# Splitting streamed weights: the low part from an accumulating transfer instead of a GpSimd subtraction

## The chip, the cores and the metric

The kernel runs on one core of one Trainium2 chip. The core has five engines with a queue each: TensorE (PE, with its weight loads shown as PEld), VectorE (DVE), ScalarE (ACT), GpSimd (POOL) and SyncE (SP), which here issues all transfers. The metric is the device time of one execution in microseconds. Before the change it is 1318.51 us (median of three runs, 1318.17 to 1319.07). The profiled execution, from which all durations below come, took 1321.76 us.

## The reference, cut to what matters

One layer of a hybrid block: 1024 latent tokens and 256 context tokens of width 1024 are normalised and modulated, and go through one input projection `w_in` (1024 x 6176). Its columns feed a gated DeltaNet with 8 heads (q, k, v, their short convolution, a gate z), a multi-scale pooling branch (u and its gate), and per-head decay numbers. An output projection, a gated residual and a last RMSNorm follow.

```
proj = einsum('bld,dp->blp', hn, w_in)              # hn: [1024 or 256, 1024]
qkv, ab, z_dn, u_pool, z_pool = split(proj)
qkv = silu(short_conv(qkv, conv_w)) ...             # 5 taps
o   = gated_delta_rule(q, k, v, g, beta, s0) ...    # context first, then latents from its state
y_pool = pool_mixer(u_pool) * silu(z_pool)
x = x + gate_x * concat(o, y_pool) @ w_out
```

All is float32. The kernel gets near that accuracy from a faster matmul type (float32r, which keeps fewer bits) by splitting each operand into a high part, rounded to float32r, and a low part, the rest: a product is then hi*hi + hi*lo + lo*hi.

## The kernel before, in words

The projection's columns are cut into 64 tiles of 128 columns: 16 for the context (k and v of each head, 256 tokens), 8 for the pooling gate, 32 for the heads (v, k, z, q of each, 1024 tokens) and 8 for u. `order` (line 654) holds their sequence, `SEQ` (line 33) its pattern: the context tiles first, with two of the gate's, then mostly the head tiles, and after the heads the eight u tiles. For each, `w_load` (line 669) brings 512 KB of raw weights to SBUF: for the first 18 tiles into two buffers in turn (`raw2`, which the profile shows as kT, and `wraw`), afterwards into `wraw` alone. `w_split` (line 679) then makes the two parts, in two halves of 4 of the 8 k-blocks. It calls `split` (line 674): ACT copies raw to the high part `whi`, and POOL subtracts, `wlo = raw - whi`. Both are double buffered. `gemm_take` starts the load of tile i+2 as tile i begins (for i below 16).

`gemm_half` (line 734) does a tile's products for up to 512 tokens in one PSUM bank: for each of 8 k-blocks three products (`PASSES`: whi*hi, whi*lo, wlo*hi), so that the third product already reads `wlo`. In its first half of the tokens it also splits the next tile's weights: the first half of the split after product 4, the second after product 14 (of 24), and from i = 16 on it issues the load of tile i+2 right behind. Tiles 0 and 1 are split earlier, between the steps of the modulation (line 1605), and tile 1 splits at products 14 and 18.

The order of all instructions is written out by a small planner, `Flow` (line 70). The gemm is its main thread. The other stages are side threads (generators): conversion and transposition of the latents (`x_half`, `x_split`), convolution of the tiles (`conv_post`), the DeltaNet's stages for two groups of context heads and for eight latent heads (`stage_a`, `stage_b`, `stage_d`, `stage_k`, `stage_q`, the scans). The planner gives each instruction a modelled cost, keeps a clock for each engine, and puts a side step into the program when its modelled inputs are due; flags (`flow.flag`, `yield ("name", n)`) order the threads. It does not model one engine slowing another. After the heads, `mix_all` and `pool_out` do the pooling, and `second_half` (line 1969) prepares the second half of the output projection while the mixing runs.

The profile puts nearly all instructions on line 364, the helper that records them, and transfers on 382; so they are told apart by their tiles: `whi`, `wlo`, `wraw`, `kT`, `vT`, `qT` (convolution results, one convolution instruction reads u and one of these), `hnhi`, `hnlo` (the latents' parts), `D` (decays, and also the context's high part), `dlo`, `ws`, `rp` (pooling).

Of the kernel before, what the change touches and what calls it, by code (L numbers as in the profile page):

```python
# [11 lines left out]
ACTF = mybir.ActivationFunctionType  # L12
ALU = mybir.AluOpType
# [21 lines left out]
N2 = 18  # L35
# [9 lines left out]
WD = 0  # L45
# [3 lines left out]
GROUPS = (2, 1, 3, 0)  # L49
# [15 lines left out]
}  # L65
ISSUE = 1220.0
LANDED = 950.0


class Flow:  # L70
# [210 lines left out]
def _use(ap, write):  # L281

    t = ap.tensor
    name = t.name
    off = int(ap.offset)
    dims = [(int(q[0]), int(q[1])) for q in ap.ap]
    if name.split("_")[0] in PSUM_TAGS:
        return name, 0, P, 0, 1 << 40, True
    if name.split("_")[0] in DRAMS or name.startswith("in_") or name.startswith("out_"):
        return name, 0, 1, off, off + 1 + sum(s * (n - 1) for s, n in dims if s > 0), write  # L290
    row = _size(t)
    p, f = off // row, off % row
    return name, p, p + dims[0][1], f, f + 1 + sum(s * (n - 1) for s, n in dims[1:] if s > 0), write
# [20 lines left out]
class Engine:  # L314
# [44 lines left out]
    def __getattr__(self, op):  # L359
        f = getattr(self.real, op)  # L360

        def call(*a, **k):
            self.flow.spend(self.name, self.cost(op, a, k), self.uses(op, a, k))
            return f(*a, **k)  # L364

        return call


class Queue:
# [21 lines left out]
def kernel(  # L391
# [22 lines left out]
    flow = Flow()  # L414
    pe, act, dve, pool = (Engine(flow, e, n) for e, n in (
        (nc.tensor, "pe"), (nc.scalar, "act"), (nc.vector, "dve"), (nc.gpsimd, "pool")))
    sync = Queue(flow, nc.sync)
# [3 lines left out]
    KT = D // P  # L421
# [111 lines left out]
    for d in range(2):  # L533
        pool.memset(mask[d], 0.0)
        pool.memset(tri[d], 1.0)
        s = 1 if d == 0 else -1
# [14 lines left out]
    ps = pp_tile()  # L551
# [60 lines left out]
    for k in range(KT):  # L612
        mod_part(0, mod_ps[0], k)
        if k == 4:
            ps = pp_tile()
            pe.transpose(ps[:, 0:P], vec_row, ident)
            act.activation(out=vec[:, 16:64], in_=ps[:, 16:64], func=ACTF.Copy)
            ps = pp_tile()
# [48 lines left out]
    raws = {}  # L667

    def w_load(n):
        if n < len(order):  # L670
            t = raws[n] = raw2 if n % 2 and n < N2 else gemm.tile([P, KT, P], FP32, tag="wraw", name="wraw")
            sync.dma_start(out=t, in_=w_in_d[:, :, order[n]:order[n] + P])

    def split(raw, hi, lo, e):

        act.activation(out=hi, in_=raw, func=ACTF.Copy)
        e.tensor_tensor(out=lo, in0=raw, in1=hi, op=ALU.subtract)

    def w_split(n, part):
        if n >= len(order):  # L680
            return
        if part == 0:
            wq[n] = [gemm.tile([P, KT, P], FP32R, tag=f"w{s}", bufs=2, name=f"w{s}") for s in ("hi", "lo")]
        hi, lo = wq[n]
        s = slice(part * (KT // 2), (part + 1) * (KT // 2))
        split(raws[n][:, s, :], hi[:, s, :], lo[:, s, :], dve if n < WD and part else pool)

    arrs = [{a: const.tile([P, 16, n], FP32, name=f"{a}{i}") for a in ("ngc", "neg", "edl", "egl", "beta")}
            for i, n in enumerate((NBC, NB))]
# [44 lines left out]
    def gemm_half(i, w, src, t0, m, evac):  # L734
        ps = mm_tile()
        j = 0
        for k in range(KT):
            for a, b in PASSES:
                pe.matmul(ps[:, 0:m], w[a][:, k, :], src(b, k, t0),
                          start=(j == 0), stop=(j == 3 * KT - 1))  # L740
                j += 1
                if t0 == 0 and j == (4 if i > 1 else 14) and i:
                    w_split(i + 1, 0)
                if t0 == 0 and j == (14 if i > 1 else 18) and i:
                    w_split(i + 1, 1)
                    if i + 2 >= N2:
                        w_load(i + 2)
                yield
        evac(ps[:, 0:m], t0)

    def gemm_tile(src, n, evac):
# [636 lines left out]
    def x_half(hf):  # L1388
        for k in range(KT):
            n = hf * KT + k  # L1390
            yield TAKE
            tp = pp_tile()
            for i in range(4):
                pe.transpose(tp[:, i * P:(i + 1) * P], xs[4 * hf + i][:, k * P:(k + 1) * P], ident)
            if XACT & 4 == 0:
                yield
            if n >= len(TMP):
                yield ("split", n - len(TMP))
            if XACT & 4:
                yield "act"  # L1400
            h32 = dl_tile([P, 512], *TMP[n % len(TMP)])
            act.activation(out=h32, in_=tp, func=ACTF.Identity,
                           scale=md[:, 0, 1, k:k + 1], bias=md[:, 0, 0, k:k + 1])
            flow.give()
            flow.flag("h32", n)
            flow.add(x_split(hf, k, h32), [("h32", n)], True)

    def x_split(hf, k, h32):
        if XACT & 8:
            yield "dve"  # L1410
        dve.tensor_copy(hn[2 * hf][:, k, :], h32)
        yield
        e = dve if k % XD == 0 else pool
        e.tensor_tensor(out=hn[2 * hf + 1][:, k, :], in0=h32, in1=hn[2 * hf][:, k, :], op=ALU.subtract)
        flow.flag("split", hf * KT + k)
# [68 lines left out]
    def thread_a():  # L1484
        for k in (-5, -4, -3):
            flow.flag("merged", k)
            flow.flag("done", k)
        for k in range(-2, H):
            yield ("k", k)
            yield ("ab", k >= 0)  # L1490
            yield ("done", k - 2)
            yield from stage_a(jobs[k])

    def thread_q():
# [334 lines left out]
    def out_main():  # L1829
# [127 lines left out]
        late = []  # L1957
# [10 lines left out]

        def second_half():
            yield ("mixed",)  # L1970
            pl_p.release()
            pools["c"] = Pool(flow, tc.alloc_tile_pool(name="outc", bufs=1, side="right", reuse_waits="tile"))
            wos = {k: [ot2([P, D], f"wo{s}{n}", 1, FP32R) for s in ("hi", "lo")] for n, k in enumerate(KS[:4])}
            yield ("pool", 2)
            for t in range(2):
                y_tiles(t, 1, ot2, 2)
                y_part(t, 1, *PARTS[0])
                wo_load(KS[t], *wos[KS[t]])
            for k in KS[2:4]:
                wo_load(k, *wos[k])  # L1980
            yield ("pool", 3)
            for slot in ("zp0", "zp1"):
                free_raw(slot)
            for t in range(2):
                y_part(t, 1, *PARTS[1])
            for k in KS[4:]:
                wo_load(k, *[pb([P, D], f"d{s}", 4, FP32R) for s in ("hi", "lo")])
            yield ("wo", KS[5])
            closed.update(("zp0", "zp1", "outb"))
            while not closed.issubset(free):  # L1990
                yield ("rel", released[0])
            cols["gate"], cols["fgain"] = gate, fgain = [pb([P, D], "zp", 2) for _ in range(2)]
            sync.dma_start(out=gate, in_=gate_d.partition_broadcast(P))
            sync.dma_start(out=fgain, in_=final_gain.partition_broadcast(P))
            x_load(0)
            x_load(1)
            yield ("heads",)
            y_tiles(2, 1, oa, 3)
            for p in PARTS:
                y_part(2, 1, *p)  # L2000
            y_load(3, 0, oa, 3)
            y_load(3, 1, oa, 3)
# [80 lines left out]
```

## Time and profile before

| what | value |
|---|---|
| median of runs | 1318.51 us |
| profiled execution | 1321.76 us, of which 1320.0 us span |
| PE busy | 1212.5 us (92%) |
| DVE busy | 928.0 us (70%) |
| ACT busy | 570.8 us (43%) |
| POOL busy | 438.7 us (33%), of which wlo<-wraw,whi 158.0 us x110 |
| transfers | 123.73 MB, mean 94 GB/s |
| granted TensorE clock | 0.962 of full speed, mean |

The busy shares are means over stages that have different limits; a stage is read from a window of its own. A timeline row gives start, duration, engine and tiles, and in brackets how long the engine idled before it and what ended that. In a group of instructions the figures after the first bar are the total busy time and the mean of one in ns, those after the second the idle time of the engine just before them and what released it. Where an instruction takes longer than others of its shape, it was held up while it ran; the profile does not say by what, so the rows of the other engines at that moment are put beside it.

### The profile page before, as it was taken

Reading aid. Unit: us, or ns where it says so; the run is one execution under the profiler, and the core shown is the slowest. Engines: PE = TensorE matmul, PEld = TensorE weight load, DVE = VectorE, ACT = ScalarE, POOL = GpSimd, SP = SyncE. Lnnn points to the kernel's source line nnn. Section 1 sums busy time; section 2 is a strip of 40 time slices with the busy share of each in tenths; the row PEclk is TensorE's granted clock in tenths of the full one; section 3 lists DMA queues with packets and bytes.
Section 4 is the critical chain, followed back from the end, with each engine's and each line's share of the span. In section 5 each row is a group of like instructions: output and inputs, shape, how many; then the busy total and the mean of one; then the engine's idle time right before and its main releaser. Section 6 shows DMA issues by size and latency. Waiting matters only on the chain.

```text
span 1320.0 us, 26398 instructions
## 1 busy us (share of the span) xinstructions
PE 1212.5 (92%) x10631; PEld 977.8 (74%) x10631; DVE 928.0 (70%) x1883; ACT 570.8 (43%) x1498; POOL 438.7 (33%) x451
## 2 busy tenths in 40 slices
PE   8876699899899999999999989999999999799997
PEld 2666577677777877788778768778788777688887
DVE  4799989868886787877776867878433999724212
ACT  3466437444436547455474464643613123322110
POOL 2477433230421423314132233141215454402330
PEclk9788899899999999989999999999999899899999
DMA  9533344223121213212221131212313135565230
GB/s 329 188 99 93 86 140 125 74 57 90 37 49 48 78 42 100 58 46 80 49 83 44 41 100 41 69 63 43 103 60 109 48 104 185 199 206 157 83 112 32
DMA packets 157384, 123.73 MB, mean 94 GB/s; under 512 B 47106, under 2 KB 135115, under 8 KB 157261
## 3 DMA queue, kind: packets, MB, share of 16 engines
q1 hardware_dynamic: 157261, 122.04, 30.6%
q8 instruction: 83, 1.36, 0.4%
q14 instruction: 40, 0.33, 0.1%
HBM read 101.43 MB, written 20.60 MB: 92 GB/s over the span
## 4 chain that ended last, share of the span: by engine, by line
PE 40%; DVE 14%; ACT 6%; DMA 2%; issue 2%; POOL 2%; DVEq 0%; SPq 0%; POOLq 0%; ACTq 0%
PE mm L364 24%; PE sc L364 5%; PE o L364 4%; DVE kT L364 4%; PE pp L364 3%; PE pa L364 3%; DVE t L364 3%; DVE ws L364 3%; ACT junk L364 2%; ACT ks L364 1%; DMA D<-gscr 1%; DVE dlo L364 1%; DVE rp L364 1%; POOL wlo L364 1%; DVE zp L364 1%
## 5 line engine op out<-in xcount | busy, mean ns | idle before, releaser
L364 PE MATMUL mm<-hnhi,whi 128*128 128x512 f32 x768 | 321.0, 418 | 0.9 <-ACT whi L364 0.9
L364 PE MATMUL mm<-hnhi,wlo 128*128 128x512 f32 x768 | 316.7, 412 | 2.0 <-POOL wlo L364 2.0
L364 PE MATMUL mm<-hnlo,whi 128*128 128x512 f32 x768 | 316.9, 413 | 0.0
L364 POOL TENSOR_TENSOR wlo<-wraw,whi 128x512 fp32r<-128x512 f32 x110 | 158.0, 1442 | 337.3 <-ACT whi L364 330.5
L364 PEld LDWEIGHTS mm<-hnhi,whi 128*128 128x128 f32 x768 | 147.7, 192 | 26.8 <-issue 1.7
L364 PEld LDWEIGHTS mm<-hnhi,wlo 128*128 128x128 f32 x768 | 146.9, 191 | 26.0 <-POOL wlo L364 2.5
L364 PEld LDWEIGHTS mm<-hnlo,whi 128*128 128x128 f32 x768 | 147.6, 192 | 22.9
L364 DVE SCALAR_TENSOR_TENSOR kT<-u,cw,kT 128x512 f32<-128x512 f32 (+1 forms) x96 | 94.8, 994 | 5.3 <-ACT kT L364 1.8
L364 POOL TENSOR_TENSOR D<-D,mask 128x512 f32<-128x512 f32 x40 | 58.9, 1478 | 92.3 <-DMA D<-gscr 76.8
L364 ACT ACTIVATE y<-sc 128x256 f32<-128x256 f32 (+1 forms) x65 | 24.9, 383 | 131.3 <-PE sc L364 125.3
L364 ACT ACTIVATE u<-mm 128x512 f32<-128x512 f32 (+1 forms) x64 | 34.8, 543 | 88.3 <-PE mm L364 88.1
L364 DVE SCALAR_TENSOR_TENSOR t<-t,laneN 128x1 f32<-128x1 f32 (+4 forms) x150 | 68.0, 453 | 6.8 <-DMA laneN<-ds 2.8
L364 ACT ACTIVATE whi<-wraw 128x512 fp32r<-128x512 f32 x110 | 67.5, 633 | 1.8 <-DMA wraw<-in_w_in_dram 1.5
L364 DVE SCALAR_TENSOR_TENSOR vT<-u,cw,vT 128x512 f32<-128x512 f32 (+1 forms) x80 | 67.2, 843 | 1.5
L364 DVE TENSOR_TENSOR pw<-mm,zp 128x512 f32<-128x512 f32 (+1 forms) x12 | 8.0, 669 | 83.9 <-PE mm L364 83.9
L364 ACT ACTIVATE D<-D,ngc 128x128 f32<-128x128 f32 x160 | 53.1, 403 | 30.7 <-POOL D L364 30.7
L364 DVE SCALAR_TENSOR_TENSOR qT<-u,cw,qT 128x512 f32<-128x512 f32 (+1 forms) x80 | 63.0, 788 | 2.9 <-ACT qT L364 1.2
L364 DVE SCALAR_TENSOR_TENSOR S<-S,egl,sc 128x128 f32<-128x128 f32 x112 | 33.7, 343 | 33.4 <-PE sc L364 30.4
L364 DVE SCALAR_TENSOR_TENSOR r<-sc,neg,vn 128x128 f32<-128x128 f32 x128 | 38.7, 345 | 23.0 <-PE sc L364 22.9
L364 PEld LDWEIGHTS sc<-S,kT 128*128 128x128 f32 x256 | 36.9, 192 | 15.6 <-issue 9.1
L364 PE MATMUL mm<-D,whi 128*128 128x256 f32 x128 | 41.2, 322 | 7.3 <-DVE ks L364 4.5
L364 PE MATMUL sc<-S,kT 128*128 128x128 f32 x256 | 40.7, 282 | 7.2 <-DVE S L364 6.7
(409 smaller groups left out, 2785.5 us busy)
## 6 DMA issues: line engine op xcount, KB each, us to landing
wraw<-in_w_in_dram SPq DMA_DIRECT2D x55, 512.0 KB, 3.8
D<-gscr SPq DMA_DIRECT2D x40, 256.0 KB, 4.1
qd<-escr SPq DMA_DIRECT2D x16, 512.0 KB
kT<-in_w_in_dram SPq DMA_DIRECT2D x9, 512.0 KB, 4.0
whnhi<-in_w_mod_dram SPq DMA_DIRECT2D x8, 512.0 KB, 3.5
whnlo<-in_w_mod_dram SPq DMA_DIRECT2D x8, 512.0 KB, 9.5
D<-in_w_mod_dram SPq DMA_DIRECT2D x8, 512.0 KB, 4.9
yscr<-zs SPq DMA_DIRECT2D x8, 512.0 KB, 2.8
```

What stands on the lines that cost most here:

```text
L364: return f(*a, **k)
```

## The change

The low part is no longer subtracted by POOL. ACT writes the high part, then writes the negated high part into `wlo`, and a transfer issued from POOL's queue adds the raw weights to it in place (SBUF to SBUF, 256 KB, `accum_op=add`). In tiles from 2 on the products are reordered: first the 16 that read `whi`, then the 8 that read `wlo`; the splits of the next tile move from products 4 and 14 to 2 and 8, and with the second one the load of tile i+2 (i of 16 and more). Two threads get one more flag to wait for. The planner gets costs for the new instruction.

```diff
+ADDS = 1000.0
+ADDED = 1500.0
...
+    def add_to(self, out, in_):
+
+        u = [_use(out, True), _use(in_, False)]
+        self.flow.spend(self.name, ADDS, u)
+        self.flow.note("sync", u, self.flow.free[self.name] + ADDED)
+        return self.real.dma_start(out=out, in_=in_, accum_op=ALU.add)
...
-        split(raws[n][:, s, :], hi[:, s, :], lo[:, s, :], dve if n < WD and part else pool)
+        act.activation(out=hi[:, s, :], in_=raws[n][:, s, :], func=ACTF.Copy)
+        act.activation(out=lo[:, s, :], in_=raws[n][:, s, :], func=ACTF.Copy, scale=-1.0)
+        pool.add_to(lo[:, s, :], raws[n][:, s, :])
...
-        for k in range(KT):
-            for a, b in PASSES:
-                pe.matmul(ps[:, 0:m], w[a][:, k, :], src(b, k, t0),
-                          start=(j == 0), stop=(j == 3 * KT - 1))
-                j += 1
-                if t0 == 0 and j == (4 if i > 1 else 14) and i:
-                    w_split(i + 1, 0)
-                if t0 == 0 and j == (14 if i > 1 else 18) and i:
-                    w_split(i + 1, 1)
-                    if i + 2 >= N2:
-                        w_load(i + 2)
-                yield
+        late = [(k, p) for k in range(KT) for p in PASSES[:2]] + [(k, PASSES[2]) for k in range(KT)]
+        for k, (a, b) in late if i > 1 else [(k, p) for k in range(KT) for p in PASSES]:
+            pe.matmul(ps[:, 0:m], w[a][:, k, :], src(b, k, t0),
+                      start=(j == 0), stop=(j == 3 * KT - 1))
+            j += 1
+            if t0 == 0 and j == (2 if i > 1 else 14) and i:
+                w_split(i + 1, 0)
+            if t0 == 0 and j == (8 if i > 1 else 18) and i:
+                w_split(i + 1, 1)
+                if i + 2 >= N2:
+                    w_load(i + 2)
+            yield
...
     def x_half(hf):
...
+        flow.flag("xt", hf)
...
     def thread_a():
...
             yield ("done", k - 2)
+            yield ("xt", 0)
             yield from stage_a(jobs[k])
...
         def second_half():
             yield ("mixed",)
+            yield ("pw", GROUPS[-1])
             pl_p.release()
```

## Rows read from the trace of the kernel before

**Rows 1.** Busy time by stretch (us), all engines; (x) counts instructions.
```profile
core 0: us, PE busy (x) PEld busy (x) DVE busy (x) ACT busy (x) POOL busy (x), PEclk, DMA share, GB/s
50.00:160.00 110.00, 75.35 (x469) 68.03 (x468) 105.74 (x179) 65.70 (x158) 75.26 (x92) 0.87 0.30 85
756.00:845.00 89.00, 82.88 (x897) 68.27 (x896) 68.80 (x161) 46.57 (x137) 26.72 (x27) 0.98 0.22 62
1028.00:1100.00 72.00, 66.32 (x277) 53.51 (x276) 69.68 (x68) 15.76 (x25) 34.95 (x24) 0.95 0.25 77
```

**Rows 2.** Groups of DVE instructions, 50 to 160 us.
```profile
L364 DVE SCALAR_TENSOR_TENSOR kT<-u,cw,kT 128x256 f32<-128x256 f32 x28 | 18.5, 660 | 2.5 <-ACT kT L364 1.8
L364 DVE SCALAR_TENSOR_TENSOR vT<-u,cw,vT 128x256 f32<-128x256 f32 x16 | 15.3, 956 | 0.4
L364 DVE SCALAR_TENSOR_TENSOR qT<-u,cw,qT 128x256 f32<-128x256 f32 x12 | 9.6, 802 | 0.3
L364 DVE CAST hnhi<-XT 128x512 fp32r<-128x512 f32 x4 | 6.2, 1554 | 0.0
...
L364 DVE CAST hnhi<-tmp 128x512 fp32r<-128x512 f32 x4 | 4.0, 1003 | 0.2 <-ACT tmp L364 0.2
...
L364 DVE CAST hnhi<-W 128x512 fp32r<-128x512 f32 x4 | 2.7, 683 | 0.0
...
L364 DVE CAST hnhi<-Y 128x512 fp32r<-128x512 f32 x4 | 2.6, 638 | 0.0
```

**Rows 3.** Timelines of DVE, POOL and SP, 89 to 102 us.
```profile
92.78 4.71 DVE L364 SCALAR_TENSOR_TENSOR vT<-u,cw,vT 128x256 f32<-128x256 f32 x4
97.42 0.41 DVE L364 CAST hnhi<-Y 128x512 fp32r<-128x512 f32 x1
...
100.96 1.52 DVE L364 SCALAR_TENSOR_TENSOR kT<-u,cw,kT 128x256 f32<-128x256 f32 x3
...
94.36 2.85 POOL L364 TENSOR_TENSOR wlo<-kT,whi 128x512 fp32r<-128x512 f32 x2
...
97.24 0.37 SPq L382 DMA_DIRECT2D kT<-in_w_in_dram  x1
```

**Rows 4.** The same stretches, instructions on wlo alone: PE, PEld, POOL.
```profile
50.00:160.00 110.00, 41.20 (x125) 26.59 (x124) 42.14 (x30) 0.87 0.30 85
756.00:845.00 89.00, 26.30 (x64) 12.09 (x64) 10.70 (x9) 0.98 0.22 62
1028.00:1100.00 72.00, 30.26 (x76) 14.53 (x76) 20.25 (x10) 0.95 0.25 77
```

**Rows 5.** Groups of PE and of ACT, 50 to 160 us.
```profile
L364 PE MATMUL mm<-D,wlo 128*128 128x256 f32 x109 | 34.7, 319 | 4.0 <-POOL wlo L364 3.2 <-POOL u L364 0.7
...
L364 ACT ACTIVATE whi<-wraw 128x512 fp32r<-128x512 f32 x16 | 9.7, 621 | 0.0
```

**Rows 6.** Transfers: issuer, count, KB each, median us from issue to landing.
```profile
wraw<-in_w_in_dram SPq DMA_DIRECT2D x55, 512.0 KB, 3.8
D<-gscr SPq DMA_DIRECT2D x40, 256.0 KB, 4.1
...
B<-in_x_dram SPq DMA_DIRECT2D x4, 512.0 KB, 8.4
```

**Rows 7.** Timelines of ACT and PE, 28 to 40 us.
```profile
30.92 1.14 ACT L364 ACTIVATE whi<-wraw 128x512 fp32r<-128x512 f32 x2
...
36.15 0.28 PE L364 MATMUL mm<-D,wlo 128*128 128x256 f32 x1
36.27 0.28 PE L364 MATMUL mm<-D,whi 128*128 128x256 f32 x1
```

**Rows 8.** Chain of waits, 756 to 845 us: start, us, what.
```profile
756.22 1.42 POOL wlo L364
757.64 1.62 POOL sm L364
```

**Rows 9.** Timelines of DVE and POOL, 1028 to 1100 us.
```profile
1048.26 1.16 DVE L364 TENSOR_TENSOR dlo<-ws,dhi 128x1024 fp32r<-128x1024 f32 x1
...
1061.95 2.31 DVE L364 TENSOR_TENSOR dlo<-ws,dhi 128x1024 fp32r<-128x1024 f32 x1
...
1058.87 4.31 POOL L364 TENSOR_TENSOR wlo<-wraw,whi 128x512 fp32r<-128x512 f32 x2 [7.70 <-ACT whi L364]
```

## The prediction

> **What bounds the kernel now.** I began with busy time by stretch, since the shares over the whole span mix stages. It shows three kinds of stage [rows 1]. From 50 to 160 us, where the context tiles and the conversion of the latents run, DVE is busy 105.74 of 110 us and PE only 75.35: DVE bounds the front. In a head's stretch (756 to 845 us; the eight heads repeat it) PE is busy 82.88 of 89 us and DVE 68.80: PE bounds, and 6.1 us a head are idle. From 1028 to 1100 us, the mixing of the pooling branch, DVE is busy 69.68 of 72 us and PE 66.32: DVE again, with PE close behind.
>
> The second view was the groups of DVE instructions in the front [rows 2], because an engine that is busy 96% may be working or held. The reader should compare the mean of a group with an undisturbed one of the same shape. Three convolution steps in a row took 1.52 us, 0.51 us each, where POOL ran nothing large; four of them took 4.71 us, 1.18 each, while POOL subtracted two halves of weights (2.85 us, from 94.36) [rows 3]. A cast of 128x512 took 0.41 us when undisturbed [rows 3], and its four groups have means of 638 to 1554 ns [rows 2]. So POOL's large two-input instructions hold DVE up, and DVE's busy time in the front contains waiting. POOL is busy 75.26 us there [rows 1], 42.14 of it on 30 subtractions for `wlo` [rows 4].
>
> The waits that the change names directly are small: PE waited 3.2 us for `wlo` in the front's context products [rows 5].
>
> **The change part by part.** It removes POOL's subtraction, adds an ACT copy and a transfer for each half tile, and moves the products and splits.
>
> *Front, what POOL gives back to DVE.* The 56 convolution steps of [rows 2] sum to 43.4 us; undisturbed they would take 56 x 0.51 = 28.6, so 14.8 are waiting. The 16 casts sum to 15.5 us against 16 x 0.41 = 6.6: 8.9 more. Together 23.7 us. I give `wlo` its share of POOL's busy time, 42.14 of 75.26 or 56%: 13.3 us. The bounds are 0 (the instruction that issues a transfer holds DVE just as long as the subtraction did) and 23.7 (with fewer large POOL instructions the rest no longer meets DVE either). DVE then needs 105.7 - 13.3 = 92.4 us; at its present 96% the stretch would be 96 us.
>
> What is late next is ACT. It has 65.70 us of work there and gets 30 copies more of 0.621 us [rows 5], 18.6 us: 84.3 of 96, 88% instead of 60%. DVE waits little for ACT at present (2.5 us before its largest group [rows 2]); with a queue that full it will wait more, and I let that take a quarter. Front: **-10 us**.
>
> The Trainium skill (page "SBUF — State Buffer", section "Who interferes with whom") adds what no row here shows: a DVE instruction with two SBUF inputs contends with a GpSimd one that reads SBUF, not with one that only writes it, while a DVE cast in a two-port mode contends with either. The trace agrees with the first half, 1.18 against 0.51 us. By the rule the convolution steps' part of the waiting goes wholly and the casts' part does not: 56% of 14.8, less the same quarter, would make the front -6 instead of -10.
>
> *Start.* Tiles 0 and 1 keep the old order of products, and the first product that reads `wlo` starts at 36.15 us [rows 7]. ACT's eight copies now follow one another from 30.92 us at 0.57 us each (1.14 for two [rows 7]), so the low copy of tile 0's first half ends at 32.1 and that of tile 1's first half, the sixth, at 34.3. The landing of such a transfer is not in the trace. The nearest row is the other one of 256 KB, 4.1 us; beside a busy stream of loads 512 KB took 8.4 us [rows 6]. With 4.1 tile 0 is just in time (36.2) and tile 1, whose first low product comes 12 products of 0.12 us later at 37.6, waits until 38.4; with 8.4 it waits until 42.7. PE goes on to the modulation, on which the latents wait, so this is on the path: 0 to +5, and with the shorter row and a little for the busy stream **+2 us**. (The skill's page "DMA: Bandwidth & Descriptors", section "Anatomy of one DMA — SWDGE (gpsimd) path", gives 2.0 us plus bytes over 436 GB/s; its estimate of 2.6 us would make this term 0.)
>
> *Middle, 160 to 1028 us.* PE's products are the same number, and `wlo` is now read 16 products later, so no PE wait is added as long as a landing takes less than a tile. ACT has 8 copies more a head, 5.0 us on 46.57 of 89 [rows 1, 5]: covered by PE's work. On the chain POOL's subtraction of 1.42 us stands ahead of the small power instruction that follows it [rows 8]; the transfer's issue takes its place and starts one ACT copy (0.62) later. If issuing is free, 0.8 us a head are gained, if it costs what the subtraction did, 0.6 are lost: times eight, -6 to +5. From tile 16 on SP issues the load of tile i+2 when the raw buffer is free, now after a landing instead of a subtraction: about 4 us more in which SP's later transfers (decay rows, the small solves' round trips) wait behind it, eased by the earlier split. PE's gemm covers that; without the cover it is inside the +5. I take **0**.
>
> *Mixing.* In 72 us there are 10 subtractions, 20.25 us of POOL [rows 4]. A `dlo` that met a pair took 2.31 us against 1.16, with POOL's pair at 4.31 [rows 9]: 1.15 us of DVE for each of five pairs, 5.8 us. PE is 92% busy beside it and takes a third back: **-4 us** (-6 to +3, the upper end if the single raw buffer, now freed by a landing, delays a u tile).
>
> *New flags.* The context's `stage_a` waits for the first eight transposes; DVE's backlog covers it. `second_half` waits for the last pooling weights, which come from the pool it releases, so they are loaded ahead of it already. Both at 0; without cover a few us, inside the bounds above.
>
> *Sum.* +2 - 10 + 0 - 4 = -12. The profiled execution of 1321.76 us becomes 1309.8; it stood 3.25 us above the median, so the median becomes **1306.5 us**. The likeliest case's own range is 1295 to 1318 (front -6 to -16, the others at half their bounds).
>
> **The rivals.**
>
> *The raw buffer's loop decides (slower).* In the front SP's load starts the moment POOL's subtraction ends, 94.36 + 2.85 = 97.21 against 97.24 [rows 3]: the buffer, not the queue, releases it. After the change one round of a buffer is the load (3.8), four ACT copies (2.5), the issue (priced as the subtraction, 1.4) and the landing L, for two tiles. Fifteen tiles in 110 us are 7.3 us each. With L = 4.1 the round is 11.8, or 5.9 a tile, and hidden under the forecast's 6.7; from L = 5.7 it eats into the gain, and above about 7 the front is longer than before. With L = 8.4 it is 8.05 a tile, 121 us: +11, with +5 at the start and -4 in the mixing, 1330 us. For it: a transfer issued from POOL has no row, and that stream will share the engines with loads. Against it: DMA engines are busy only 0.30 in the front [rows 1]. 20%.
>
> *DVE gets everything.* The whole 23.7 us of waiting goes, ACT keeps up, and the mixing gives 6: -28 with the start, 1290 us. For it: DVE's idle time before its groups is a few us in 110. Against it: POOL's other large instructions (33 us) remain. 13%.
>
> *The issue holds DVE as the subtraction did.* Front and mixing 0, start +2, middle anywhere within its bounds: 1320 us. For it: the rows can't say which part of a POOL instruction holds DVE. 12%, divided evenly over the three signs.
>
> **How the numbers follow.** The forecast holds 55%. Of it 51 points are faster, 3 within, 1 slower, 0.2% (2.6 us) being what a measurement of this kernel can tell. With 13 points from the second rival, 4, 4 and 4 from the third, and 20 slower from the first: faster 0.68, same 0.07, slower 0.25. The range of 1289 to 1328 takes in the second rival's middle and most of the first's.
>
> **What the profile will show.** If I am right: no group `wlo<-wraw,whi` on POOL, an ACT group of 128 low copies near 0.62 us, convolution steps in the front near 0.5 to 0.7 us instead of 0.66 to 0.96, the front's end about 10 us earlier, heads of 88 to 90 us, landings of the new transfer below 5 us. I am wrong if the steps keep their means (the issue holds DVE), if ACT waits for raw loads in the front (the loop), or if a head's stretch changes by more than a microsecond.

## The result and the profile after

The changed kernel takes 1364.1 us (median of 4 runs, 1358.5 to 1366.5) against 1318.3 us before in the same comparison (4 runs): a ratio of 1.034, 95% interval 1.031 to 1.037. It is 46 us slower where 12 us faster was forecast, outside the range. Its profiled execution took 1358.46 us, 1356.7 of it span; it is the fastest of its four, and that of before stood above its median, so the two traces differ by 36.7 us where the medians differ by 45.8.

The page's first part shows that the engines do what the prediction wanted of them. These are busy time, share of the span and instructions:

```profile
PE 1230.9 (91%) x10631; PEld 987.7 (73%) x10631; DVE 852.8 (63%) x1883; ACT 635.4 (47%) x1626; POOL 356.1 (26%) x451
```

VectorE has lost 75 us of busy time (928.0 before), GpSimd 83 (438.7), and ScalarE has gained 65. The windows that answer to [rows 1], a head and the mixing at their later places, show where it went wrong:

```profile
core 0: us, PE busy (x) PEld busy (x) DVE busy (x) ACT busy (x) POOL busy (x), PEclk, DMA share, GB/s
50.00:160.00 110.00, 74.17 (x415) 64.95 (x413) 71.18 (x156) 65.97 (x152) 46.70 (x80) 0.75 0.66 142
808.50:895.30 86.80, 82.92 (x893) 67.56 (x893) 63.11 (x160) 49.65 (x143) 22.06 (x26) 0.98 0.39 87
1074.00:1146.00 72.00, 70.78 (x311) 58.01 (x310) 63.31 (x83) 24.72 (x40) 19.93 (x25) 1.00 0.60 158
```

In the front nothing is busy any more: DVE fell from 105.74 to 71.18 of 110 us, yet fewer DVE instructions ran (156 against 179) and fewer of PE's (415 against 469). A head and the mixing look as hoped, the head with 86.8 us instead of 89 even more than the microsecond that the forecast allowed. The convolution steps did become shorter, as these groups of DVE in the front show beside [rows 2] (660, 956 and 802 ns there):

```profile
L366 DVE SCALAR_TENSOR_TENSOR kT<-u,cw,kT 128x256 f32<-128x256 f32 x28 | 13.5, 484 | 6.0 <-ACT kT L366 5.1
L366 DVE SCALAR_TENSOR_TENSOR vT<-u,cw,vT 128x256 f32<-128x256 f32 x16 | 9.5, 596 | 0.5
L366 DVE SCALAR_TENSOR_TENSOR qT<-u,cw,qT 128x256 f32<-128x256 f32 x12 | 7.6, 636 | 0.8 <-DVE qT L366 0.5
```

To find the lost time I marked six points in the two timelines and took the differences (us; worked out from the starts of instructions in one execution, the fifth mark from an end). The first mark is the end of the context's modulation, the second the last context product, the third and fourth the stores of the first and the eighth head's output, the fifth the last pooling product of the streamed weights.

| stretch | before | after | difference |
|---|---|---|---|
| start to modulation | 41.6 | 52.1 | +10.5 |
| to the last context product | 123.9 | 151.6 | +27.7 |
| to the first head's store | 259.6 | 248.6 | -11.0 |
| to the eighth head's store | 582.3 | 598.5 | +16.2 |
| to the last pooling product | 110.7 | 99.7 | -11.0 |
| to the end | 202.0 | 206.3 | +4.3 |

The three middle stretches together are 5.8 us shorter: work moved between them. By these sums the 36.7 us of the two traces are the front's 38.2; that a shorter front would give them back does not follow (see ctx_old). Its first 10.5 are plain in the timeline: PE waits at the first product of tile 0 and again of tile 1 that reads `wlo` (start, us, what; in brackets the idle time before, and who ended it):

```profile
31.86 1.97 POOL L375 DMA_DIRECT2D wlo<-wraw  x2 [2.14 <-ACT wlo L366]
33.91 0.83 POOL L375 DMA_DIRECT2D wlo<-kT  x1
...
39.92 0.58 PE L366 MATMUL mm<-D,wlo 128*128 128x256 f32 x1 [4.13 <-DMA wlo<-wraw]
...
45.13 0.58 PE L366 MATMUL mm<-D,wlo 128*128 128x256 f32 x1 [2.27 <-DMA wlo<-kT]
```

In [rows 7] the first of these started at 36.15. Transfers issued at 31.86 and 33.91 were waited for until 39.9 and 45.1, 8 and 11 us. They run while x and the weights are loaded. Over 37 to 52 us the DMA share is 1.02, so the DMA engines are full, and after the waits PE is granted little more than its lower clock, 1.2 GHz (0.54; 0.78 before, the second line):

```profile
37.00:52.00 15.00, 9.80 (x38) 6.52 (x38) 0.00 (x0) 1.07 (x2) 0.00 (x0) 0.54 1.02 303
```

```profile
37.00:52.00 15.00, 13.61 (x72) 9.90 (x71) 6.79 (x20) 6.43 (x15) 2.67 (x5) 0.78 0.63 230
```

Over the whole kernel such a transfer lands as forecast in the median; these are the issues beside [rows 6] (count, KB, median us to landing):

```profile
wlo<-wraw POOLq DMA_DIRECT2D x110, 256.0 KB, 3.7
wlo<-kT POOLq DMA_DIRECT2D x18, 256.0 KB, 4.6
...
B<-in_x_dram SPq DMA_DIRECT2D x4, 512.0 KB, 11.0
```

The other 27.7 us have another look. The planner wrote another order: the first transpose of x stands behind 189 context products (135 before), the context's `stage_a` behind all 336 of those written there (219 before), and so do the second half's transposes (237 before). With those 336 gone, the next tile in `order` is one of the gate, which needs the latents that this chain converts; so there is nothing left to fill PE while the chain runs.

### The profile page after: what moved, and what is told of

Read it like the earlier page. It is cut to its first block, busy times and chain, and to the rows that moved or that the text cites. A ratio compares the mean times of both kernels' runs of the same rounds, so it can differ in the third digit from the quotient of the medians.

```text
span 1356.7 us, 26753 instructions
## 1 busy us (share of the span) xinstructions
PE 1230.9 (91%) x10631; PEld 987.7 (73%) x10631; DVE 852.8 (63%) x1883; ACT 635.4 (47%) x1626; POOL 356.1 (26%) x451
## 4 chain that ended last, share of the span: by engine, by line
PE 39%; ACT 5%; DVE 5%; POOL 3%; DMA 3%; issue 2%; SPq 0%; DVEq 0%; POOLq 0%; ACTq 0%
PE mm L366 24%; PE sc L366 5%; PE o L366 4%; PE pp L366 3%; DMA D<-gscr 3%; PE pa L366 2%; ACT junk L366 2%; POOL qd L366 1%; DVE t L366 1%; DVE ws L366 1%; POOL D L366 1%; DVE rp L366 1%; ACT B L366 1%; ACT VV L366 1%; DVE qT L366 0%
## 5 line engine op out<-in xcount | busy, mean ns | idle before, releaser
L366 PE MATMUL mm<-hnhi,wlo 128*128 128x512 f32 x768 | 228.6, 415 | 0.0
L375 POOL DMA_DIRECT2D wlo<-wraw x110 | 97.2, 892 | 477.9 <-ACT wlo L366 285.2
L366 PEld LDWEIGHTS mm<-hnhi,wlo 128*128 128x128 f32 x768 | 138.4, 191 | 24.9 <-issue 1.6
L366 DVE SCALAR_TENSOR_TENSOR kT<-u,cw,kT 128x512 f32<-128x512 f32 (+1 forms) x96 | 62.9, 660 | 14.6 <-ACT kT L366 11.2
L366 ACT ACTIVATE wlo<-wraw 128x512 fp32r<-128x512 f32 x110 | 69.2, 629 | 0.0
L366 DVE SCALAR_TENSOR_TENSOR qT<-u,cw,qT 128x512 f32<-128x512 f32 (+1 forms) x80 | 57.9, 731 | 3.0 <-DVE qT L366 0.5
L366 DVE SCALAR_TENSOR_TENSOR t<-t,laneN 128x1 f32<-128x1 f32 (+4 forms) x150 | 51.8, 345 | 11.3 <-DMA laneN<-ds 7.2
L366 DVE SCALAR_TENSOR_TENSOR vT<-u,cw,vT 128x512 f32<-128x512 f32 (+1 forms) x80 | 56.9, 718 | 2.2
L366 PE MATMUL mm<-D,wlo 128*128 128x256 f32 x128 | 31.6, 362 | 26.2 <-DMA wlo<-wraw 21.0
L366 DVE SCALAR_TENSOR_TENSOR D<-pp,sm,D 128x128 f32<-128x128 f32 x128 | 35.6, 344 | 22.4 <-PE pp L366 22.4
```

What stands on the lines that cost most here:

```text
L375: return self.real.dma_start(out=out, in_=in_, accum_op=ALU.add)
```

## The experiments

Each kernel ran beside the kernel before on one chip; ratios are to that. In the first four expectations A is the theory that the transfer's latency costs the time and B that the planner's costs for it do; from the fifth on the letters are given anew in each text.

**start_old.** The changed kernel, with tiles 0 and 1 split by GpSimd's subtraction:

```
+        if n < 2:
+            split(raws[n][:, s, :], hi[:, s, :], lo[:, s, :], pool)
+            return
```

> The changed kernel, but tiles 0 and 1 are split as before (POOL subtracts). Theory A, the landing of the adding transfer is what costs (12.7 us beside the loads of the start, 3.7 elsewhere): the two waits at the start go, the modulation's last values come at 42 us instead of 52, the time falls by about 10 to 1354, and the context stage from there stays as long as it is (about 150 us). Theory B, the order that the planner writes is what costs, not the waits: the context stage has slack for the start, and the time stays within 4 us of 1364.

Measured: 1353.9 us, ratio 1.027 (1.023 to 1.030). The start's 10 us are the transfer's; the rest stays.

**ctx_old.** The same with `n < N2`, the 18 context tiles.

> The changed kernel, but the 18 tiles up to the end of the context are split as before; the 46 others use the adding transfer. Both theories: the loss lies in the front alone, which goes back to its length of before (last context product near 166 us). What is left is the change's effect on the heads and the mixing: I expect 1308 to 1315, 4 to 10 us faster than before, from less waiting of VectorE in the mixing. If the middle loses by ScalarE's additional copies or SP's longer waits, it is 1320 to 1330.

Measured: 1349.3 us, 1.023 (1.020 to 1.026). A miss: the transfer in the front was supposed to carry the rest, and taking it out there gave back under 5 us more. In its trace the front is 16.5 us shorter than in start_old, but the two stretches behind it are together 12.9 longer.

**all_sub.** The changed kernel without any transfer or second copy; the late products (the eight that read `wlo`, put at a tile's end), the moved splits and both flags stay:

```
-        act.activation(out=lo[:, s, :], in_=raws[n][:, s, :], func=ACTF.Copy, scale=-1.0)
-        pool.add_to(lo[:, s, :], raws[n][:, s, :])
+        pool.tensor_tensor(out=lo[:, s, :], in0=raws[n][:, s, :], in1=hi[:, s, :], op=ALU.subtract)
```

> Only the order of the products, the earlier splits and the new flags: every low part is subtracted by POOL as before, without additional copies and transfers. Theory A: as before, 1314 to 1322. If the reordering or the flags (the context's stage waits for the first eight transposes) make the front longer: 1335 or more, and the transposes of the latents lie behind the context tiles here too.

Measured: 1350.9 us, 1.024 (1.020 to 1.028). So 32 us are lost with no transfer in the kernel at all.

**old_plan.** The changed kernel's instructions, the planner charged as if GpSimd subtracted (1223 ns, no landing, no second copy).

> The changed kernel, but its planner is given the costs of the subtraction (1223 ns on POOL, no second ScalarE copy, no landing), so that it writes nearly the order that it would write for the subtraction; the instructions are those of the change. Theory B: the latents' transposes lie between the context tiles again (first near 75 to 85 us), and the time falls to 1325 to 1335, the rest being the start. Theory A: the waits are physical, the engines' queues stall in any order, and the time stays at 1350 or more.

Measured: 1416.0 us, 1.074 (1.070 to 1.078). Hiding the real costs from the planner is worse by 52 us; theory B fell in this form.

**dma_alone and dma_heads.** From the other side: the kernel before with the transfer as its only edit, for all tiles and for those behind the context. The planner knows of it and writes its own order.

> The kernel before with one edit alone: each streamed tile's low part comes from ScalarE's negated copy and the adding transfer, all 64 tiles; products in the old order, splits at the old points (4 and 14), neither new flag. Written down in this program: first transpose of x's first half behind 105 context products (135 before, 189 changed), the context's stage_a behind 213 (219 before, 336 changed), the second half's transposes from 205 (237 before, 336 changed). Theory A (the order of the instructions that the other edits bring costs the time, the transfer only about 10 us at the start): 1305 to 1328, the start's +10 less what a freed VectorE gives back. Theory B (the transfer and the raw buffers' loop of 6 us a tile cost it, whatever the order): 1335 or more.

> The same single edit for the 46 tiles behind the 18 of the context; those 18 are split by GpSimd as before. The order written down for the whole front is that of the kernel before (135, 219, 237). Theory A: 1300 to 1316, no start, no new order, VectorE freed in the mixing and beside the heads. Theory B: the transfer's latency costs in the heads too, 1319 or more.

Measured: 1358.8 us, 1.032 (1.029 to 1.035), and 1342.2 us, 1.020 (1.017 to 1.023). Both miss theory A. In dma_alone the front is 9.5 us longer, all of it the start, though its transposes stand earlier than before; the heads' stretch takes 619 us against 582. "Late transposes in the front cost the time" is thus not the whole of it.

**late_sub and moves_sub.** No transfer; of the order's edits, the late products with both flags, or the moved splits with both flags. (The late products without the flags were not tried, so the flags' share in late_sub is open.)

> No transfer at all: GpSimd subtracts as before and splits stand at the old points; of the change only the late products and the two new flags. Written down: first transpose of x behind 175 context products, context's stage_a behind 309, second half's transposes behind all 336. Theory A: between 1335 and 1351, near the run that had all four edits without the transfer (1350.9). Theory B: 1316 to 1322, no change.

> No transfer: GpSimd subtracts as before, products in the old order; of the change only the splits moved to products 2 and 8 and the two new flags. Written down: first transpose of x behind 174 context products, stage_a behind 291, second half's transposes from 327. Theory A: 1330 to 1350, as the positions are nearly those of the late products' run. If the late products are the only costly edit: 1316 to 1325.

Measured: 1336.9 us, 1.013 (1.009 to 1.018), and 1372.7 us, 1.043 (1.040 to 1.045). One half of the edits costs 20 us, the other 56, all four together 32: they don't add up, since each gives the planner another order to write.

**Order and transfer apart.** So I froze the order. The planner's charges can be kept while the instruction that is issued is exchanged; every queue then holds the same instructions in the same order but for the exchange. That gives the other corners of a square. In the old order:

```
         act.activation(out=hi[:, s, :], in_=raw, func=ACTF.Copy)
+        nc.scalar.activation(out=lo[:, s, :], in_=raw, func=ACTF.Copy, scale=-1.0)
+        flow.spend("pool", 1223.2, [_use(lo[:, s, :], True), _use(raw, False), _use(hi[:, s, :], False)])
+        nc.gpsimd.dma_start(out=lo[:, s, :], in_=raw, accum_op=ALU.add)
```

and in the changed kernel's order the reverse: charged as copy and transfer, issued as a subtraction.

> The transfer without any new order: on every engine's queue the instructions stand word for word as in the kernel before, save that each subtraction on GpSimd has become the issue of the adding transfer in the same place, with ScalarE's negated copy right behind its first copy; no late products, no moved splits, no flags. Theory A (the order costs the time): 1310 to 1332, the start's 10 at most and what a freed VectorE gives back. Theory B (the transfer's own latency and ScalarE's second copy cost it): 1345 or more.

> The other corner: the changed kernel's instructions in its own order on every queue, but each adding transfer is GpSimd's subtraction again in the same place, without ScalarE's second copy. Theory A: 1340 to 1360, nearly the changed kernel's 1364 less the start's 10. Theory B: 1315 to 1325.

| time, us (ratio, interval) | subtraction | transfer |
|---|---|---|
| old order | 1317.4 | 1348.3 (1.025, 1.019 to 1.030) |
| new order | 1350.1 (1.023, 1.020 to 1.027) | 1364.1 (1.034, 1.031 to 1.037) |

Neither theory alone holds. The order by itself costs 33 us, the transfer by itself 31, and together 46, as the transfer adds only 14 in the new order.

The new order without the transfer has its last context product 22.2 us later than before (187.7 against 165.5). Its windows show the hole:

```profile
50.00:120.00 70.00, 49.42 (x349) 47.14 (x347) 62.68 (x93) 37.51 (x91) 44.37 (x59) 0.87 0.36 100
120.00:155.00 35.00, 11.16 (x50) 8.68 (x49) 30.96 (x63) 21.96 (x57) 20.23 (x24) 0.60 0.22 57
155.00:188.00 33.00, 26.24 (x355) 21.05 (x354) 17.34 (x42) 8.96 (x20) 10.40 (x13) 0.81 0.25 65
```

From 120 to 155 us PE works 11.16 of 35 us at a granted clock of 0.60, and DVE is busy for 30.96: the chain of transposes, casts and `stage_a` runs with no products left to lie beside it. The waits of PE in that stretch go from one engine to the next:

```profile
PE pp L366 <- DVE ks L366: 4.9, 1, 4.9
PE pp L366 <- DVE qd L366: 4.9, 2, 2.7
PE pp L366 <- ACT Y L366: 4.6, 1, 4.6
PE pa L366 <- ACT vn L366: 4.2, 1, 4.2
```

**Where the transfer's 31 us lie in the old order.** Two more kernels leave the transfer out for tiles 0 and 1, and for all 18 tiles up to the context's end.

> The same in the old order, but tiles 0 and 1 are split by GpSimd as before. Theory A: about 10 under the run with all tiles, 1300 to 1322. Theory B: 1335 or more.

> The same in the old order with the transfer only for the 46 tiles behind the context's 18. The heads with the transfer in an order of their own gave 1342. Theory A: 1305 to 1319. Theory B: 1330 to 1345, the heads' stretch as long as in that run (606 us against 582).

Measured: 1339.2 us, 1.016 (1.012 to 1.019), and 1338.5 us, 1.015 (1.010 to 1.020). By differences the start takes 9 us, tiles 2 to 17 1, and the 46 tiles behind the context 21 (13 to 26 by the interval). The heads' stretch is not the 606 us that theory B had, it is 582.4 against 582.3 before; the loss lies elsewhere. The 21 us got two runs of their own: one with ScalarE's second copy and no transfer, one with the transfer and the raw load later in SP's queue (charged at its old place, noted in `pend`, and issued further on).

```
 copy_heads, behind the high copy:
+        nc.scalar.activation(out=lo[:, s, :], in_=raw, func=ACTF.Copy, scale=-1.0)
         pool.tensor_tensor(out=lo[:, s, :], in0=raw, in1=hi[:, s, :], op=ALU.subtract)
 late_load_heads, the load of the tile after the next:
+                if t0 and j == 8 and pend:
+                    nc.sync.dma_start(out=pend[0][0], in_=pend.pop()[1])
```

> The order of the kernel before on every queue and GpSimd's subtraction everywhere; for the 46 tiles behind the context ScalarE makes the negated copy too, into the low part, which the subtraction then overwrites. No transfer. Theory C1 (ScalarE's second copy is what the transfer costs in the heads, 92 copies of 0.63 us, 58 us in a queue whose results TensorE waits for): 1333 to 1343, as the run with the transfer in these tiles in the old order (1338.5). Theory C2 (the raw buffer is held until the transfer has landed, and SP's queue behind it) and C3 (the transfers' traffic): 1316 to 1323.

> The transfer for the 46 tiles behind the context, old order, but the next tile's raw load stands later in SP's queue: at the 8th product of the tile's second half, 18 products further on, so that SP waits less for the buffer that the transfer still reads and reaches its other loads sooner. The 18 late products are about 4 us of TensorE. Theory C2: 1318 to 1330, and the waits of TensorE for S from DRAM (11.8 us in the heads) gone. C1 or C3: 1335 to 1345, or more if the raw tile itself comes late.

Measured: copy_heads 1315.3 us, 0.998 (0.997 to 1.000); late_load_heads 1322.7 us, 1.005 (1.003 to 1.007). The group of these extra copies is ScalarE's 92 instructions:

```profile
L691 ACT ACTIVATE wlo<-wraw 128x512 fp32r<-128x512 f32 x92 | 58.0, 631 | 0.0
```

58 us of added work cost nothing, and moving the load gave back 16 of the 21 us by the medians (14 by the means; the four runs of oldorder_heads spread from 1331 to 1344). That is theory C2, with one detail of it wrong: TensorE's waits for `S` from DRAM did not go (11.8 us in the heads, 12.3 with the late load). What changed lies ahead of them. From the last context product to the first head's store the three traces take 259.6 (before), 269.3 (oldorder_heads) and 260.0 us (late_load_heads). In that stretch DVE's waits for loads, ScalarE's for the lane tiles (`laneN`, what comes back from small round trips through DRAM) and SP's for the raw buffer are (total, times, longest; before, then oldorder_heads, then late_load_heads):

```profile
DVE D L364 <- DMA D<-in_w_mod_dram: 4.4, 3, 3.6
DVE t L364 <- DMA laneN<-ds: 1.7, 2, 1.4
ACT W L364 <- DMA laneN<-vs: 1.7, 1, 1.7
SPq L382 <- POOL wlo L364: 87.0, 8, 24.8
```

```profile
DVE D L364 <- DMA D<-in_w_mod_dram: 12.0, 4, 4.4
DVE t L364 <- DMA laneN<-ds: 6.1, 3, 3.2
ACT W L364 <- DMA laneN<-vs: 6.1, 2, 3.9
SPq L382 <- DMA wlo<-wraw: 147.4, 12, 28.3
```

```profile
DVE D L364 <- DMA D<-in_w_mod_dram: 6.1, 2, 4.3
DVE t L364 <- DMA laneN<-ds: 2.3, 2, 1.9
SPq L766 <- DMA wlo<-wraw: 103.5, 9, 30.8
```

SP issues its transfers in turn. While it waits for the raw buffer, which the adding transfer reads until it lands, the modulation weights and lane tiles behind it are late, and they come back to time when the raw load stands further on; ScalarE then has no wait for the lane tiles left. (The profiled oldorder_heads is its fastest of four, so the trace shows 10 of the median's 21 us. What the last 5 us are is open.)

**oldorder_ctx.** The transfer for tiles 2 to 17 alone, in the old order, tests the prediction's gain where it was forecast.

> The transfer for tiles 2 to 17 alone, in the old order: neither the start nor the heads have it. This is the only stretch where VectorE bounds and waits for GpSimd's subtraction, so if any version gains it is this one. From the two runs with tiles 2 to 63 and 18 to 63 (1339.2 and 1338.5) the sixteen tiles cost nothing: 1313 to 1321. If the raw buffers' loop of about 6 us a tile counts by itself: 1322 to 1330.

Measured: 1321.9 us, 1.003 (1.000 to 1.005): no gain, and between the two ranges. From 50 to 160 us its window and groups are:

```profile
50.00:160.00 110.00, 76.01 (x469) 70.34 (x467) 84.99 (x187) 80.23 (x187) 60.95 (x92) 0.86 0.74 156
```

```profile
L364 DVE SCALAR_TENSOR_TENSOR kT<-u,cw,kT 128x256 f32<-128x256 f32 x28 | 16.8, 599 | 4.3 <-ACT kT L364 3.7
L364 DVE SCALAR_TENSOR_TENSOR qT<-u,cw,qT 128x256 f32<-128x256 f32 x12 | 8.6, 717 | 0.3
L364 DVE SCALAR_TENSOR_TENSOR vT<-u,cw,vT 128x256 f32<-128x256 f32 x16 | 7.7, 482 | 1.9 <-ACT vT L364 1.4
...
L364 PE MATMUL mm<-D,wlo 128*128 128x256 f32 x109 | 37.0, 339 | 26.6 <-DMA wlo<-kT 17.5 <-DMA wlo<-wraw 9.1
```

DVE has 21 us less to do for the same instructions, but PE now stands 26.6 us before its low products (4.0 in [rows 5]), and the last context product starts at 165.5 us, as before. The stall went from DVE to PE.

The same trace answers whether the issue holds DVE as the subtraction did. Between 50 and 165 us, 15 convolution steps and two casts met nothing of GpSimd's but an issue. They took 0.47 to 0.49 us and 0.42 and 0.45, as undisturbed ones do [rows 3]. Every step or cast that still took over 0.9 us met a two-input instruction of GpSimd's. Three steps beside two issues:

```profile
76.21 1.52 DVE L364 SCALAR_TENSOR_TENSOR kT<-u,cw,kT 128x256 f32<-128x256 f32 x3
...
75.83 0.86 POOL L693 DMA_DIRECT2D wlo<-wraw  x1 [3.70 <-ACT u L364]
77.17 0.85 POOL L693 DMA_DIRECT2D wlo<-wraw  x1 [0.48 <-ACT wlo L691]
```

**moves_alone and moves_undone.** Which edit makes the order costly? The moved splits were added alone to the kernel before, and alone undone in the changed kernel:

```
-                if t0 == 0 and j == (4 if i > 1 else 14) and i:
+                if t0 == 0 and j == (2 if i > 1 else 14) and i:
...
-                if t0 == 0 and j == (14 if i > 1 else 18) and i:
+                if t0 == 0 and j == (8 if i > 1 else 18) and i:
```

> One edit of the order by itself: the splits at products 2 and 8 in place of 4 and 14; subtraction on GpSimd, old product order, no flags. Written down: first transpose of x behind 174 context products, stage_a behind 243 (219 before, 291 with the flags), second half's transposes from 315 (327 with the flags). Theory A1 (the moved splits cost it, as they stand in GpSimd's queue ahead of what the heads need): 1355 to 1375, near the 1372.7 with the flags. Theory A2 (the flag on x's transposes costs it): 1318 to 1335.

> The changed kernel with one part undone: the splits stand at products 4 and 14 again. The transfer, the late products and both flags stay. Theory A1 (the moved splits are the costly edit of the order in the changed kernel too): 1325 to 1345, 20 to 40 under the changed kernel's 1364. If the moves and the flags each bring about the same late order (stage_a still stands behind all 336 context products here): 1350 to 1365.

Measured: 1365.1 us, 1.036 (1.034 to 1.039), and 1369.7 us, 1.040 (1.037 to 1.042). Alone the moves cost 47 us. The flags beside them add about 8 (1372.7 in moves_sub). Undone in the changed kernel they give nothing back; 1369.7 lies above both ranges. In moves_alone the front is only 5 us longer, but the stretches to the first and to the eighth head's store are 20.5 and 14.2 longer, and in the heads PE has a wait that the kernel before does not have at all:

```profile
PE o L364 <- POOL qd L364: 15.1, 6, 4.4
```

Theory A1's reason was a subtraction standing ahead of what the heads need. Its time came true, but the trace of moves_alone shows something else at the longest of these waits (rows of GpSimd, then of PE):

```profile
463.25 0.24 POOL L364 TENSOR_SCALAR sm<-sm 128x8 f32<-128x8 f32 x1 [2.66 <-DVE sm L364]
463.58 1.68 POOL L364 TENSOR_TENSOR sm<-sm,expo 128x8 f32<-128x8 f32 x1
465.23 4.65 POOL L364 TENSOR_TENSOR qd<-qd,qT 128x1024 f32<-128x1024 f32 x2
...
467.63 0.80 PE L364 MATMUL o<-S,qd 128*128 128x128 f32 x2 [4.45 <-POOL qd L364]
```

Ahead of `qd` stands the small power instruction `sm`, which waited for DVE, and so it is at the other waits (645.6 and 821.6 us). In the kernel before a subtraction stands directly ahead of `qd` in five of the seven heads after 425 us, and PE does not wait. So the planner's order of the heads' stages changed. No run put `sm` back, so what this costs is not shown. The second moved split also takes the load of tile i+2 with it, and no run parted the two. What is shown is that no one edit carries the order's cost: five kernels without the transfer, with different sets of these edits, end 20 to 56 us later.

**late_load_before.** A version that could beat both: the kernel before with only the raw load later in SP's queue.

> A version that could beat both: the kernel before with GpSimd's subtraction, and only the raw load of the 46 tiles behind the context later in SP's queue (8th product of the second half). SP stood 406.6 us behind GpSimd's subtraction in the kernel before, 275.5 of it in the heads, so its other loads could gain as they did with the transfer. Theory C2, if SP's order is a limit with the subtraction too: 1303 to 1314. If the subtraction frees the buffer soon enough: 1315 to 1322.

Measured: 1317.0 us, 1.000 (0.998 to 1.002). So with the subtraction the place of the raw load in SP's queue is no limit. No version here beats the kernel before by more than 0.3%; copy_heads, the lowest, is 0.2% under it with work that serves nothing.

## Why the prediction was wrong

- **New flags, "both at 0", and the order as a whole: the step that failed.** "DVE's backlog covers it" took the planner's order as given. The planner prices every operation and writes the order of all queues from that, so a changed price, a moved split or a flag can move thousands of instructions. The sum had no term for it. Measured without the transfer: +33 us. The trace has the front 22.2 us longer, where `stage_a` and the second half's transposes ended up behind 336 of the context's products, and 7.5 us more behind it. The flags' own share is open (beside the moved splits about 8 us).
- **Start, +2: right mechanism, wrong size.** It is +9 to +10 by two differences (1364.1 less 1353.9; 1348.3 less 1339.2), and in the traces of all five kernels with the transfer on tiles 0 and 1 the modulation ends 9.3 to 10.5 us later. I took the landing's shorter row, 4.1 us; the loads of x stand beside it, and it took 8 and 11. The row with 8.4 [rows 6], named as the other end, was the nearer one, and I left out that PE then runs on at the lower clock.
- **Front, -10: the cause was right, the gain wasn't there.** In the old order the 56 convolution steps of oldorder_ctx sum to 33.1 us against 43.4, and its 16 casts to 10.2 against 15.5: 15.6 us came back, where 13.3 were forecast. The issue on GpSimd doesn't hold DVE (15 steps and two casts beside an issue alone took their undisturbed time), and that rival fell. (The Trainium skill, page "SBUF — State Buffer", section "Who interferes with whom", agrees for the convolution steps; it would have left the casts' waiting, and there 5.3 us went.) The share of 56% was an assumption that came out near: the 4.71 us of [rows 3] that the forecast put down to the subtraction met another two-input instruction first, `D<-D,mask`, 1.48 us from 92.92. But DVE's 96% did not make it the only limit. With DVE freed, PE waited 26.6 us for `wlo`. The late products did not take that wait away: in the changed kernel PE waits 19.7 us for `wlo` between the first two marks, 27.1 in oldorder_ctx and 5.2 before. Whether the front would be shorter with DVE freed and no such wait, no run shows.
- **ACT, "a quarter": too little in the old order.** DVE waited 3.3 us for ACT in the front before, 21.2 in oldorder_ctx.
- **Middle, 0.** The forecast named SP's later transfers behind the held buffer and said "PE's gemm covers that". In the old order it does not: of the 21 us that the 46 tiles behind the context cost, 16 came back with the load further on, and the trace has its share ahead of the first head's store. The bound of +5 was too small, as it was counted for PE's products and not for the loads that DVE and ScalarE wait for between them. In the changed kernel the two stretches to the eighth head's store are together 5.2 us longer than before, but 7.9 in the same order without the transfer (neworder_sub): there the transfer cost nothing.
- **Mixing, -4.** In the old order with the transfer everywhere the stretch from the eighth head's store to the last pooling product is 109.5 us against 110.7: -1. DVE was freed there too (59.96 of 72 us, 1051 to 1123), but PE stayed as busy as before (66.60; 66.32 in [rows 1]). In the changed kernel the stretch is 11.0 us shorter, and 6.5 shorter in the same order without the transfer: there the transfer gave 4.5, as forecast, and PE at 70.78 of 72 us bounds.
- **The raw buffers' loop** runs near what was computed (5.9 us a tile): ScalarE's first copies begin 6.4 us a tile apart between 61 and 138 us, and ScalarE now waits 19.9 us for raw tiles in the front where it waited for none. It isn't what made the front late: without any transfer the front already ends 22.2 of its 38.2 us later, the start takes 10.6, and 5.4 are left for the loop and all else.

Of the chance of 25% for slower, 20 points were that loop's, 4 the third rival's and 1 the forecast's own. A rival in which the order itself changes stood nowhere.

## What to carry to other kernels

Where a program writes the order of a kernel's instructions from prices, an edit is two edits: the operation, and the order that follows. Price and test them apart, by keeping the charges while the operation is exchanged, and the reverse. When a transfer takes an engine's place, it holds its source until it lands; look for the in-order queue that waits for that buffer, and at what stands behind it. And an engine freed is not time gained until the next wait is read: here 21 us of DVE's busy time went, and PE waited 27 us for the transfer that freed it.

## What the runs showed of the hardware

- The issue of a 256 KB adding transfer keeps GpSimd busy for 0.87 us in the median, and the transfer lands 3.8 us after it in the median of all 128, 3.2 at the least and 12.7 at the most, which is one of the start's four. The Trainium skill, page "DMA: Bandwidth & Descriptors", section "Anatomy of one DMA — SWDGE (gpsimd) path", would estimate it at 2.6 by its formula; no landing here was that short:

```profile
L375 POOL DMA_DIRECT2D wlo<-wraw x110: 841/869/1240, 31.9 to 1129.1; - x110
...
DMA to landing us min/median/max: 3.2/3.8/12.7
```

- An issue of that transfer does not hold VectorE: convolution steps beside it took 0.47 to 0.49 us, beside two-input instructions of GpSimd's up to 3.3 us (oldorder_ctx).
- ScalarE took 58 us of further copies for the 46 tiles behind the context at no cost that can be measured (0.998, 0.997 to 1.000).
